# Hybrid encoder trunk on one core: the gated convolution inside the attention stage, its sums on GpSimd, its column tiles in another order

## The chip, the cores and the metric

The kernel runs on one core of one Trainium2 chip. Its engines are TensorE (PE; PEld is its weight load), VectorE (DVE), ScalarE (ACT), GpSimd (POOL) and SyncE (SP, which issues the DMAs here). The metric is the device time of one execution in microseconds (us), as the median of several runs.

## The reference

Two layers over 1024 positions of 1024 channels, float32. Each mixes three head groups side by side, then runs a convolutional gated MLP:

```python
h = rmsnorm(x, norm1_g); p = h @ w_in
q, k, v, su, sv, cb, cc, cx = split(p, (512, 128, 128, 256, 256, 256, 256, 256))
a_out = softmax_attention(rope(rmsnorm(q)), rope(rmsnorm(k)), v)      # 8 heads, 2 KV heads
g_out = su * (sg_w @ rmsnorm(sv) + sg_b)                              # chunks of 128 positions
c_out = cb * dwconv3(cc * cx, conv_w)                                 # 256 channels
x = x + concat(a_out, g_out, c_out) @ w_out
x = x + (silu(g) * u) @ ffn_w_down,   [g, u] = dwconv3(rmsnorm(x) @ ffn_w_up)
# dwconv3(x, w)[t] = x[t-1] * w[0] + x[t] * w[1] + x[t+1] * w[2]
```

The change concerns `c_out` alone: three projections (C = `cc`, X = `cx`, gate = `cb`) and a three-tap convolution along the positions.

## The kernel before

Every float32 product is made from high and low parts: an operand is split into `h` (a rounded copy) and `l` (the rest), and three matmuls hh, hl, lh add up in PSUM. `split` does this: the copy (L106 on ACT, L110 on POOL), then the subtraction (L117 on DVE or POOL).

**The attention stage.** Per layer there are 16 units `u` (128 queries by one of the two KV groups, four heads `r` each). `attention` (L654) writes TensorE's order out by hand, under a manual schedule for TensorE alone; a scheduler orders the other engines. In each of eight positions `kc` of a unit it issues: the transposes of the previous unit's probabilities (`att_T`, L622, four of 128x128 into a bank of the PSUM pair `pa`, split from there by ACT L626 and DVE L627); in positions 0, 1, 3 and 4 one head's scores (`att_scores`: matmuls L605 and L606, maximum on DVE L608, exponential on ACT L611, reciprocal on DVE L613, and the scaling of the probabilities by it on POOL, L614); some filler matmuls; and the product with V (L634, L635) of the hl pair made two positions earlier. The first transposes of a unit read all four heads of the unit before, so they need its fourth L614. DVE L649 and L650 end a unit's output.

**The filler** is the generator `conv_steps` (L454): the gated convolution's 288 matmuls of a layer (L301), one for each step. It goes over six column tiles of 128 channels, `order`, each as two halves of 512 positions, 24 matmuls a half, all into the one PSUM bank `pf`. For the channels j = 0, 1 the tiles come in turn as C, X, gate. A C half is copied out by ACT (L473) into `cc` (buffer G1); an X half is multiplied into it by DVE (L475), and after the second half `conv3` makes the three-tap sum: ACT L438 writes t = w1 * u, then DVE L439 and L443 add the two shifted products, each over 1023 positions in one instruction. A gate half is multiplied into t by DVE (L480). Steps are drawn at FILL: 16 ahead of unit 0, 32 in it, 12 in each unit 1 to 15, 24 in the unit 16 (which only transposes and multiplies with V), and the remaining 36 after it. So the second tile, X of channels 0, ends with unit 4; the fourth ends with unit 12; the fifth ends half-way through unit 16.

**Weights.** `cw_load` brings the next tile's 512 KB by DMA into buffer E5 (the first tile's into E8) and POOL splits them into G6/W0 or G7/W3 in turn. E5 is handed from one tile to the next, and after the last to a slice of the output projection's weights (`load_wo0`), whose second slice goes to G1, where `cc` has been. ACT and DVE or POOL split these slices into H0 and H1, the buffers of the probabilities, when attention has read them for the last time. SP issues DMAs in one queue, in the scheduler's order.

Of the kernel before, what the change touches and what calls it, by code (L numbers as in the profile page):

```python
# [10 lines left out]
AF = mybir.ActivationFunctionType  # L11
ALU = mybir.AluOpType
# [4 lines left out]
NT = 1024  # L17
# [5 lines left out]
C_K, C_SU, C_CB, C_CC, C_CX = 512, 768, 1280, 1536, 1792  # L23
# [33 lines left out]
class Trunk:  # L57
# [351 lines left out]
    def sg_half(self, half):  # L409
# [22 lines left out]
            nc.scalar.activation(B[:, kc, :], acc, AF.Copy)  # L432
        self.mB[half] = B

    def conv3(self, t, u, w):

        nc = self.nc
        nc.scalar.activation(t, u, AF.Copy, scale=w[1])  # L438
        nc.vector.scalar_tensor_tensor(  # L439
            out=t[:, 1:NT], in0=u[:, 0 : NT - 1], scalar=w[0], in1=t[:, 1:NT],  # L440
            op0=ALU.mult, op1=ALU.add,
        )
        nc.vector.scalar_tensor_tensor(  # L443
            out=t[:, 0 : NT - 1], in0=u[:, 1:NT], scalar=w[2], in1=t[:, 0 : NT - 1],
            op0=ALU.mult, op1=ALU.add,
        )
# [7 lines left out]
    def conv_steps(self, L, hT):  # L454

        nc = self.nc
        order = [(j, c) for j in range(2) for c in (C_CC, C_CX, C_CB)]
        self.mC = [None, None]
        W = {0: self.cw_load(L, order[0][1], 0)}
        for n, (j, c) in enumerate(order):  # L460
            if n + 1 < len(order):
                j2, c2 = order[n + 1]
                W[n + 1] = self.cw_load(L, c2 + j2 * P, n + 1)
            if c == C_CC:
                cc = self.S("G1")
            elif c == C_CX:
                t = self.mC[j] = self.S(("Z0", "Z1")[j])
            for half in range(2):
                s = slice(half * 512, half * 512 + 512)
                pm = self.acc("pf")  # L470
                yield from self.chan_mm_steps(pm, hT, half, W[n])
                if c == C_CC:
                    nc.scalar.activation(cc[:, s], pm, AF.Copy)  # L473
                elif c == C_CX:
                    nc.vector.tensor_tensor(out=cc[:, s], in0=pm, in1=cc[:, s], op=ALU.mult)  # L475
                    if half == 1:
                        w = [self.cst[:, 88 + 2 * k + j : 89 + 2 * k + j] for k in range(3)]
                        self.conv3(t, cc, w)
                else:
                    nc.vector.tensor_tensor(out=t[:, s], in0=pm, in1=t[:, s], op=ALU.mult)  # L480
                yield
# [800 lines left out]
```

## Time and profile before

| | |
|---|---|
| median of 3 runs | 2242.65 us (2241.32 to 2243.2) |
| profiled execution, its own time | 2240.78 us |
| its span (first to last instruction) | 2239.0 us |
| granted TensorE clock, mean | 0.998 |
| busy: PE / DVE / ACT / POOL | 99% / 68% / 49% / 51% of the span |
| attention stages | about 142 to 395 us and 1251 to 1506 us |

The busy shares are of the whole span; a stage can have another limit. The lists of waits say what ended the idle time of an engine; "A <- B: 6.6, 4, 2.0" is 6.6 us in all, four times, the longest 2.0 us.

### The profile page before, as it was taken

How to read it: one execution, taken by the hardware profiler on the slowest of the kernel's cores; microseconds unless marked ns; L12 is line 12 of the kernel's file. 1: busy time of each engine (PE TensorE's matmuls, PEld its weight loads, DVE VectorE, ACT ScalarE, POOL GpSimd, SP SyncE). 2: the span in 40 equal slices, each digit the busy share in tenths (PEclk: the TensorE clock that was granted, in tenths of full speed). 3: DMA queues.
4: the chain of work that ended last, by engine and by line, in shares of the span. 5: the costliest groups of instructions: out<-in, count | busy, mean ns of one | idle time of the engine just before them, and what ended most of it. 6: DMA issues, size and time to landing. Idle time of an engine off the chain costs nothing.

```text
span 2239.0 us, 29385 instructions
## 1 busy us (share of the span) xinstructions
PE 2206.4 (99%) x10590; PEld 1830.0 (82%) x10590; DVE 1530.1 (68%) x1953; ACT 1107.5 (49%) x1879; POOL 1130.9 (51%) x1028
## 2 busy tenths in 40 slices
PE   9999999999999999999999999999999999999999
PEld 7887887877888888888888878878788888888887
DVE  6568887278687777754735688872777777778554
ACT  4247776265454444433422467763555454444332
POOL 5463335587777777020443633356777777751100
PEclk9999999999999999999999999999999999999999
DMA  4110002223555453886520000032235554548754
GB/s 160 42 29 10 11 10 85 104 76 101 163 161 169 151 168 121 296 314 215 198 90 10 29 10 11 10 106 92 77 112 160 168 157 160 165 141 316 282 192 163
DMA packets 202019, 281.90 MB, mean 126 GB/s; under 512 B 15598, under 2 KB 121618, under 8 KB 201874
## 3 DMA queue, kind: packets, MB, share of 16 engines
q1 hardware_dynamic: 201874, 280.03, 37.2%
q8 instruction: 83, 1.36, 0.2%
q14 instruction: 62, 0.51, 0.1%
HBM read 199.77 MB, written 80.22 MB: 125 GB/s over the span
## 4 chain that ended last, share of the span: by engine, by line
PE 87%; DVE 5%; POOL 2%; DMA 2%; issue 2%; ACT 2%; SPq 0%; POOLq 0%; DVEq 0%; ACTq 0%
PE pa L860 18%; PE pf L860 9%; PE big L1059 8%; PE pa L1059 5%; PE pf L301 5%; PE pa L622 5%; PE po L860 4%; PE po L1059 3%; PE pf L1059 3%; PE big L606 3%; PE big L605 3%; PE po L634 2%; PE po L635 2%; PE pa L132 2%; PE pa L131 2%; PE pa L130 2%
## 5 line engine op out<-in xcount | busy, mean ns | idle before, releaser
L614 POOL TENSOR_SCALAR H<-H,rv 128x1024 f32<-128x1024 f32 x128 | 144.8, 1131 | 269.6 <-DVE rv L613 269.6
L860 PE MATMUL pa<-H,E 128*128 128x512 f32 x864 | 212.8, 390 | 1.4 <-DVE H L893 1.4
L106 ACT ACTIVATE E<-E 128x512 fp32r<-128x512 f32 (+1 forms) x207 | 128.5, 628 | 159.2 <-POOL E L848 69.8
L627 DVE TENSOR_TENSOR E<-pa,E 128x512 fp32r<-128x512 f32 x256 | 173.3, 688 | 48.1 <-ACT E L626 46.6
L117 POOL TENSOR_TENSOR E<-E,E 128x512 fp32r<-128x512 f32 (+1 forms) x120 | 176.0, 1471 | 51.0 <-ACT E L106 50.6
L626 ACT ACTIVATE E<-pa 128x512 fp32r<-128x512 f32 x256 | 152.9, 597 | 87.9 <-PE pa L622 86.6
L860 PEld LDWEIGHTS pa<-H,E 128*128 128x128 f32 x864 | 161.6, 188 | 35.7 <-DVE H L893 2.3
L106 ACT ACTIVATE G<-H 128x1024 fp32r<-128x1024 f32 (+1 forms) x116 | 114.1, 1008 | 143.3 <-PE big L1059 71.9
L117 DVE TENSOR_TENSOR G<-H,G 128x1024 fp32r<-128x1024 f32 (+1 forms) x86 | 104.6, 1220 | 109.4 <-ACT G L106 109.1
L622 PEld LDWEIGHTS pa<-ident,H 128*128 128x128 f32 x1024 | 127.4, 141 | 42.7 <-issue 4.7
L622 PE MATMUL pa<-ident,H 128*128 128x128 f32 x1024 | 154.3, 273 | 6.7 <-DVE E L627 6.6
L608 DVE TENSOR_REDUCE nm<-big 128x1 f32<-128x1024 f32 x128 | 155.6, 1216 | 6.3 <-PE big L606 6.2
L894 ACT ACTIVATE H<-pa 128x512 f32<-128x512 f32 x128 | 75.8, 593 | 166.4 <-PE pa L860 121.3
L611 ACT ACTIVATE H<-big,nm 128x1024 f32<-128x1024 f32 x128 | 142.4, 1113 | 18.0 <-DVE nm L608 17.9
L301 PE MATMUL pf<-H,G 128*128 128x512 f32 x320 | 130.4, 428 | 1.6 <-DVE Z L480 1.6
L439 DVE SCALAR_TENSOR_TENSOR big<-H,cst,big 128x1023 f32<-128x1023 f32 x44 | 56.6, 1287 | 102.2 <-ACT big L438 102.2
L117 DVE TENSOR_TENSOR E<-E,E 128x512 fp32r<-128x512 f32 (+1 forms) x92 | 97.3, 1066 | 39.3 <-ACT E L106 38.8
L860 PE MATMUL pa<-W,E 128*128 128x512 f32 x336 | 116.0, 394 | 0.8 <-ACT H L894 0.5
L106 ACT ACTIVATE G<-E 128x512 fp32r<-128x512 f32 (+2 forms) x110 | 58.5, 547 | 99.1 <-POOL E L848 29.8
L978 POOL TENSOR_TENSOR E<-E 128x512 f32<-128x512 f32 x26 | 35.3, 1360 | 140.0 <-DMA E<-in_ffn_w_down_dram 139.7
L860 PE MATMUL po<-H,E 128*128 128x512 f32 x408 | 104.4, 390 | 0.4 <-ACT E L106 0.4
L634 PE MATMUL po<-E,E 128*128 128x512 f32 x256 | 101.0, 394 | 2.2 <-DVE E L650 2.2
(400 smaller groups left out, 6353.5 us busy)
## 6 DMA issues: line engine op xcount, KB each, us to landing
H<-gdram SPq DMA_DIRECT2D x70, 512.0 KB, 5.6
gdram<-H SPq DMA_DIRECT2D x134, 256.0 KB, 2.4
E<-in_ffn_w_up_dram SPq DMA_DIRECT2D x66, 512.0 KB, 4.4
H<-tdram SPq DMA_DIRECT2D x40, 512.0 KB, 5.7
E<-in_w_in_dram SPq DMA_DIRECT2D x30, 512.0 KB, 3.9
H<-in_ffn_w_down_dram SPq DMA_DIRECT2D x30, 512.0 KB, 4.7
out_dram<-H SPq DMA_DIRECT2D x28, 512.0 KB, 2.9
E<-in_ffn_w_down_dram SPq DMA_DIRECT2D x26, 512.0 KB, 6.6
```

Source lines behind the costliest of these rows:

```text
L106: nc.scalar.activation(out, in_, AF.Copy)
L117: e.tensor_tensor(out=l, in0=src, in1=h.bitcast(F32), op=ALU.subtract)
L301: mm(acc, a[:, k, :], b, start=k + j == 0, stop=k == KC - 1 and j == 2)
L608: nc.vector.tensor_reduce(out=nm, in_=S, op=ALU.max, axis=AX.X, negate=True)
L611: nc.scalar.activation(p, S, AF.Exp, bias=nm, accum_out=sm)
L614: nc.gpsimd.tensor_scalar(out=p, in0=p, scalar1=rv, scalar2=1.0, op0=ALU.mult, op1=ALU.mult)
L622: nc.tensor.transpose(pt[:, r * P : (r + 1) * P], pu[:, r, kc * P : (kc + 1) * P], self.ident)
L626: nc.scalar.activation(hl[:, 0, :], pt, AF.Copy)
L627: nc.vector.tensor_tensor(out=hl[:, 1, :], in0=pt, in1=hl[:, 0, :].bitcast(F32), op=ALU.subtract)
L634: self.nc.tensor.matmul(O, v, hl[:, 0, :], start=kc == 0, stop=False)
L860: mm(out, w, x, start=first and k + j == 0, stop=k == 3 and j == 2, skip_group_check=True,)
L1059: nc.tensor.matmul(banks[j], p[:, n, s], r[:, n, :], start=first and n + q == 0 and m < 3, stop=last and n == w - 1 and q == 2, skip_group ...
```

## The change

A new function `conv3_pool` stands in for `conv3` in the attention stage: ACT still writes t = w1 * u, and GpSimd makes, for each half of the positions and each of the two outer taps, a scaled shifted copy in a temporary (buffer E5) and adds it to t, eight instructions instead of DVE's two. The tiles come as C, X, C, X, gate, gate. The second half of the first tile and of the last goes to a `pa` bank.

```diff
+    def conv3_pool(self, t, u, w):
+        self.nc.scalar.activation(t, u, AF.Copy, scale=w[1])
+        tmp = self.S("E5")
+        for a, b in ((0, 512), (512, NT)):
+            for o, k in ((-1, 0), (1, 2)):
+                lo, hi = max(a, -o), min(b, NT - o)
+                src, dst = tmp[:, lo:hi], t[:, lo:hi]
+                self.nc.gpsimd.tensor_scalar(
+                    out=src, in0=u[:, lo + o : hi + o], scalar1=w[k], scalar2=1.0,
+                    op0=ALU.mult, op1=ALU.mult,
+                )
+                self.nc.gpsimd.tensor_tensor(out=dst, in0=src, in1=dst, op=ALU.add)
...
-        order = [(j, c) for j in range(2) for c in (C_CC, C_CX, C_CB)]
+        order = [(j, c) for j in range(2) for c in (C_CC, C_CX)] + [(0, C_CB), (1, C_CB)]
...
-                t = self.mC[j] = self.S(("Z0", "Z1")[j])
+                self.mC[j] = self.S(("Z0", "Z1")[j])
+            t = self.mC[j]
...
-                pm = self.acc("pf")
+                pm = self.acc("pa" if half and n in (0, 5) else "pf")
...
-                        self.conv3(t, cc, w)
+                        self.conv3_pool(t, cc, w)
```

Lines behind the new function stand 16 later in the changed kernel (L614 is L630, L627 is L643). The order of three engines moves where the prediction speaks of it. On GpSimd, at the end of unit 4 of the first layer, before (H0 and H1 are the probabilities of even and odd units, E5 the raw weights):

```order
L614 TENSOR_SCALAR H0_404_2106<-H0_404_2106,rv_432_2210 128x1024
L110 TENSOR_SCALAR G7_447_2280<-E5_446_2278 128x1024
L117 TENSOR_TENSOR W3_448_2281<-E5_446_2278,G7_447_2280 128x1024
L614 TENSOR_SCALAR H1_439_2257<-H1_439_2257,rv_445_2275 128x1024
L614 TENSOR_SCALAR H1_439_2257<-H1_439_2257,rv_456_2310 128x1024
L614 TENSOR_SCALAR H1_439_2257<-H1_439_2257,rv_465_2344 128x1024
L614 TENSOR_SCALAR H1_439_2257<-H1_439_2257,rv_471_2368 128x1024
```

and now (Z0 is t, G1 is u, cst holds the taps):

```order
L443 TENSOR_SCALAR E5_439_2251<-G1_269_1539,cst_125_645 128x512
L447 TENSOR_TENSOR Z0_298_1667<-E5_439_2251,Z0_298_1667 128x511
L447 TENSOR_TENSOR Z0_298_1667<-E5_439_2251,Z0_298_1667 128x512
L443 TENSOR_SCALAR E5_439_2251<-G1_269_1539,cst_125_645 128x512
L443 TENSOR_SCALAR E5_439_2251<-G1_269_1539,cst_125_645 128x511
L447 TENSOR_TENSOR Z0_298_1667<-E5_439_2251,Z0_298_1667 128x512
L447 TENSOR_TENSOR Z0_298_1667<-E5_439_2251,Z0_298_1667 128x511
L630 TENSOR_SCALAR H1_440_2264<-H1_440_2264,rv_446_2282 128x1024
L630 TENSOR_SCALAR H1_440_2264<-H1_440_2264,rv_458_2318 128x1024
L630 TENSOR_SCALAR H1_440_2264<-H1_440_2264,rv_467_2352 128x1024
L110 TENSOR_SCALAR G7_448_2287<-E5_447_2285 128x1024
L630 TENSOR_SCALAR H1_440_2264<-H1_440_2264,rv_473_2376 128x1024
```

Seven of the convolution's eight instructions stand in one block between units 4 and 5 (the first stands two units earlier), and the split of the next weights has moved from ahead of unit 5's scalings to either side of the fourth of them. The same rows come at unit 12, and both again in layer 1.

On VectorE, at the same place before:

```order
L475 TENSOR_TENSOR G1_269_1539<-pf_372_1968,G1_269_1539 128x512
L627 TENSOR_TENSOR E8_438_2244<-pa_437_2239,E8_438_2244 128x512
L439 SCALAR_TENSOR_TENSOR Z0_298_1667<-G1_269_1539,cst_125_645,Z0_298_1667 128x1023
L608 TENSOR_REDUCE nm_443_2271<-big_442_2266 128x1
L627 TENSOR_TENSOR E6_441_2263<-pa_440_2258,E6_441_2263 128x512
L443 SCALAR_TENSOR_TENSOR Z0_298_1667<-G1_269_1539,cst_125_645,Z0_298_1667 128x1023
L649 TENSOR_TENSOR E1_373_1972<-po_420_2166,ot_450_2288 64x2x128
L650 TENSOR_TENSOR E1_373_1972<-po_420_2166,ot_450_2288 64x2x128
```

and now:

```order
L491 TENSOR_TENSOR G1_269_1539<-pf_372_1968,G1_269_1539 128x512
L643 TENSOR_TENSOR E8_438_2244<-pa_437_2239,E8_438_2244 128x512
L624 TENSOR_REDUCE nm_444_2278<-big_443_2273 128x1
L643 TENSOR_TENSOR E6_442_2270<-pa_441_2265,E6_442_2270 128x512
L665 TENSOR_TENSOR E1_373_1972<-po_420_2166,ot_452_2296 64x2x128
L666 TENSOR_TENSOR E1_373_1972<-po_420_2166,ot_452_2296 64x2x128
```

The two sums are gone between the product (L475, now L491) and the unit's maxima and subtractions; nothing else changes place.

On ScalarE, at the end of unit 15, before (H0 is free once unit 15 has transposed it):

```order
L626 ACTIVATE E6_852_3948<-pa_851_3943 128x512
L106 ACTIVATE H0_874_4119<-E5_876_4121 128x1024
L626 ACTIVATE E7_854_3962<-pa_853_3957 128x512
L647 ACTIVATE ot_855_3970<-po_834_3870 64x256
L648 ACTIVATE ot_855_3970<-po_834_3870 64x256
L626 ACTIVATE E8_857_3980<-pa_856_3975 128x512
```

and now:

```order
L106 ACTIVATE H0_876_4133<-E5_878_4135 128x1024
L106 ACTIVATE H0_876_4133<-G1_879_4137 128x1024
L642 ACTIVATE E7_856_3979<-pa_855_3974 128x512
L663 ACTIVATE ot_857_3987<-po_836_3887 64x256
L664 ACTIVATE ot_857_3987<-po_836_3887 64x256
L642 ACTIVATE E8_859_3997<-pa_858_3992 128x512
```

The second weight slice's copy (from G1) has come forward, ahead of unit 16's first copy out of `pa`; before, it waited for `conv3` of the channels 1 to release G1.

## Rows read from the trace of the kernel before

**Rows 1.** The page: busy time of each engine, and the chain's shares by engine.
```profile
PE 2206.4 (99%) x10590; PEld 1830.0 (82%) x10590; DVE 1530.1 (68%) x1953; ACT 1107.5 (49%) x1879; POOL 1130.9 (51%) x1028
...
PE 87%; DVE 5%; POOL 2%; DMA 2%; issue 2%; ACT 2%; SPq 0%; POOLq 0%; DVEq 0%; ACTq 0%
```
**Rows 2.** Waits of TensorE, whole span: us in all, times, longest.
```profile
PE pa L622 <- DVE E L627: 6.6, 4, 2.0
PE po L634 <- DVE E L650: 2.2, 2, 1.1
PE pf L301 <- DVE Z L480: 1.6, 2, 0.8
PE pf L301 <- ACT G L473: 1.4, 2, 0.7
```
**Rows 3.** Timeline of DVE around unit 4's end: start, us, line, tiles, idle before.
```profile
212.21 0.69 DVE L475 TENSOR_TENSOR G<-pf,G 128x512 f32<-128x512 f32 x1
214.12 2.95 DVE L439 SCALAR_TENSOR_TENSOR Z<-G,cst,Z 128x1023 f32<-128x1023 f32 x1 [0.62 <-ACT Z L438]
216.99 1.21 DVE L608 TENSOR_REDUCE nm<-big 128x1 f32<-128x1024 f32 x1
218.13 0.68 DVE L627 TENSOR_TENSOR E<-pa,E 128x512 fp32r<-128x512 f32 x1
218.72 1.27 DVE L443 SCALAR_TENSOR_TENSOR Z<-G,cst,Z 128x1023 f32<-128x1023 f32 x1
```
**Rows 4.** Timeline of PE, first transposes of unit 5 and those of position 2.
```profile
212.94 0.60 PE L622 MATMUL pa<-ident,H 128*128 128x128 f32 x4
218.95 0.63 PE L622 MATMUL pa<-ident,H 128*128 128x128 f32 x4 [1.96 <-DVE E L627]
```
**Rows 5.** Stretch after the same place in layer 1: length, busy times, clock, DMA, GB/s.
```profile
1331.00:1335.00 4.00, 3.85 (x12) 3.10 (x13) 3.38 (x7) 1.69 (x3) 1.13 (x1) 0.57 0.01 4
```
**Rows 6.** Timeline of GpSimd: fourth scaling of unit 12, four of unit 13.
```profile
326.11 1.12 POOL L614 TENSOR_SCALAR H<-H,rv 128x1024 f32<-128x1024 f32 x1 [0.34 <-DVE rv L613]
333.62 1.14 POOL L614 TENSOR_SCALAR H<-H,rv 128x1024 f32<-128x1024 f32 x1 [2.88 <-DVE rv L613]
336.01 1.13 POOL L614 TENSOR_SCALAR H<-H,rv 128x1024 f32<-128x1024 f32 x1 [1.25 <-DVE rv L613]
338.29 1.13 POOL L614 TENSOR_SCALAR H<-H,rv 128x1024 f32<-128x1024 f32 x1 [1.15 <-DVE rv L613]
340.24 1.13 POOL L614 TENSOR_SCALAR H<-H,rv 128x1024 f32<-128x1024 f32 x1 [0.82 <-DVE rv L613]
```
**Rows 7.** Timeline of PE: first transposes of units 13 and 14.
```profile
327.68 0.60 PE L622 MATMUL pa<-ident,H 128*128 128x128 f32 x4
341.77 0.60 PE L622 MATMUL pa<-ident,H 128*128 128x128 f32 x4
```
**Rows 8.** Durations by line: ns min/median/max, first and last start.
```profile
L627 DVE TENSOR_TENSOR E<-pa,E x256: 669/692/694, 159.2 to 1494.5; 128x512 fp32r<-128x512 f32 x128
L439 DVE SCALAR_TENSOR_TENSOR Z<-G,cst,Z x4: 2367/2674/2958, 214.1 to 1488.5; 128x1023 f32<-128x1023 f32 x4
```
**Rows 9.** Groups of GpSimd instructions, shapes apart: busy us, mean ns, idle before.
```profile
L614 POOL TENSOR_SCALAR H<-H,rv 128x1024 f32<-128x1024 f32 x128 | 144.8, 1131 | 269.6 <-DVE rv L613 269.6
L117 POOL TENSOR_TENSOR W<-E,G 128x1024 fp32r<-128x1024 f32 x10 | 24.0, 2404 | 0.5
L978 POOL TENSOR_TENSOR E<-E,E 128x512 f32<-128x512 f32 x8 | 15.7, 1962 | 0.6
```
**Rows 10.** Timeline of ACT around unit 4's end.
```profile
212.94 1.15 ACT L438 ACTIVATE Z<-G,cst 128x1024 f32<-128x1024 f32 x1 [0.53 <-DVE G L475]
```
**Rows 11.** Timeline of ACT at the end of unit 15.
```profile
368.48 1.05 ACT L106 ACTIVATE H<-E 128x1024 fp32r<-128x1024 f32 x1
```
**Rows 12.** The page: DMA issues, KB each, median us to landing.
```profile
E<-in_w_in_dram SPq DMA_DIRECT2D x30, 512.0 KB, 3.9
E<-in_ffn_w_down_dram SPq DMA_DIRECT2D x26, 512.0 KB, 6.6
```

## The prediction

> **What bounds the kernel now.** First the page's busy times and chain: TensorE is busy 2206.4 of 2239.0 us and holds 87% of the chain [rows 1]. It is the bound, and a change is worth only the idle time (some 33 us in all) that it gives back or adds. So the next view is TensorE's own list of waits, from which I take the four lines that belong to the filler or to the attention around it [rows 2]: 6.6 us in four waits of the transposes for DVE's subtraction L627, 2.2 us in two of the product with V for DVE's L650, 1.6 us in two of the filler for DVE's gate product, 1.4 us in two for ACT's copy of a C half. Both bank waits come from `pf` being a single bank. The sum is 11.8 us, half in each layer.
>
> DVE's timeline names the cause of the first two lines [rows 3]: after unit 4 the first sum L439 takes 2.95 us and the second, L443, 1.27 us, and the maximum and the subtraction that unit 5 needs stand in the queue between and behind them. TensorE, which began unit 5 at 212.94, waits 1.96 us for the bank of position 2 [rows 4]. The other pair of such waits lies in unit 16, where the sums of the channels 1 come. In layer 1 the same stall is followed by 4 us at a mean granted clock of 0.57, that is, mostly at 1.2 instead of 2.4 GHz, with TensorE nearly always busy [rows 5]: 4.00 x (1 - 0.57) = 1.7 us more. In layer 0 the clock stays at full speed after it. So 11.8 + 1.7 = 13.5 us can be had in the profiled execution.
>
> **The change part by part.**
> *DVE loses the four pairs of sums.* Nothing on DVE takes their place, and the product ahead of them stays. The 8.8 us of the first two lines go, if nothing else makes L627 late. What is left ahead of it is ACT's scaling of 1.15 us, which stays where it was [rows 10]: it holds unit 5's first copy by some 0.4 us, and the bank concerned is asked for again only two positions later. I take no stall from it; at worst its whole length in each of four places, 4.6 us.
>
> *GpSimd gains eight instructions for each of the four sums.* No row of before shows them, so they are bounded. A scaling of 128x512: half of the 1.13 us of L614 with 1024 elements, 0.57; at most 1.13. An add of 128x512: half of the 2.40 us of the weights' subtraction of 1024 elements, 1.20; at most the 1.96 us of the slowest group of this shape [rows 9]. I take the lower ones, since the weights' subtraction runs in this very stage. The whole is 4 x (0.57 + 1.20) = 7.1 us; one scaling stands two units earlier, where GpSimd is idle for several us between units. The block of seven starts when the second half's product is done, which is when the next unit starts (product at 212.21 for 0.69 us, unit at 212.94 [rows 3, 4]). Call that T. The adds need ACT's scaling, done at T + 1.2. So the block ends at T + 1.2 + 4 x 1.20 + 2 x 0.57 = T + 7.1.
>
> What stands behind it are the next unit's four scalings L614, and TensorE needs the fourth for the first transposes of the unit after. Unit 13 of before shows when they come without disturbance [rows 6, 7]: with T = 327.68, at T + 5.9, 8.3, 10.6 and 12.6; the fourth ends at T + 13.7 and unit 14 starts at T + 14.1. Behind the block the first runs from 7.1 to 8.3, 1.2 us late; the second starts at 8.3, on time. The delay is caught up before it reaches TensorE.
>
> *The weights' split moves.* Its copy L110 now stands between the third and the fourth scaling, and its raw data cannot be loaded before the block has left E5. SP issues that DMA at T + 7.1 and it lands 3.9 us later [rows 12], at T + 11.0; the third scaling ends at 11.7, so the copy (1.1 us) runs 11.7 to 12.8 and the fourth scaling 12.8 to 13.9, 0.2 us before unit 14 needs it. So this just fits: the cover is the third scaling, and it holds as long as an add stays under some 1.35 us. At 1.42 us an add the stall would be about 0.2 us in each of four places. I take 0.1 us each, 0.4 in all. The other weights are split as before, up to four units ahead of use. In layer 0 and 1 alike SP now also loads the slice for G1 ahead of the last tile's weights; G1 comes free with the block's last scaling, 2.4 us earlier, so that DMA is half through when the second starts.
>
> *The tiles' order.* C of channels 1 writes `cc` half a tile after the first sum has read it for the last time; the gates come tens of us after their sums. No wait comes of it, and the matmuls are the same in number. G1 is released at unit 12 rather than in unit 16, so the output projection's second slice is there early. Its copy of 1.05 us now stands ahead of unit 16's first copy on ACT [rows 11], which comes 0.8 us late; the bank is asked for again at position 2, where L627 ends just in time. I take 0.3 us in each layer, 0.6 in all; at worst 1.05 each.
>
> *Two halves in `pa`.* The first tile's second half runs in unit 0, when no transposes use `pa`; the last half runs after the attention, when their last bank has long been read. Both bank waits go, 1.6 + 1.4 = 3.0 us. Before, six matmuls of the output projection stood ahead of the last product with V; now they stand behind the filler, and that product comes right when its L627 ends. I take 0.1 us a layer, 0.2 in all.
>
> *Sum:* 13.5 - 0.4 - 0.6 - 0.2 = 12.3 us. From the profiled execution's own 2240.78 us this makes 2228.5. The median of the runs is 1.87 us above that execution, so the forecast is 2230.4, said as 2230.5.
>
> A rule of the Trainium skill speaks against the change. "GPSIMD Engine Reference", section "Engine selection", gives elementwise work on a tile to VectorE, since GpSimd is about twice as slow for operations with two inputs. No run here shows the ratio for this operation; the rows agree in direction, as the subtraction L627 of 512 elements takes 0.69 us on DVE [rows 8] and half of the weights' 2.40 us is 1.20 [rows 9]. By that rule the change loses wherever the sums are waited for; by the rows GpSimd has the time and DVE has not. The last rival is what it would look like.
>
> **The rivals.**
> *Half of it stays.* DVE is still the engine that TensorE nearly waits for, and ACT's scaling and the product come at the same moment as before; a stall of about 1 us could be left at each of the four places, and 0.5 us at each of two bank waits. For it: L439 itself ran at 2.37 to 2.96 us [rows 8] where the second sum took 1.27 [rows 3], so two engines working at once can cost each other time, and GpSimd now works exactly there. Against it: L627 took between 0.669 and 0.694 us in all 256 cases [rows 8], beside GpSimd's splits too. Time: 2230.5 + 5 = 2235.5.
>
> *The stall is not the sums'.* If the DVE queue was late for another reason (the product or ACT's scaling), only the bank waits go: 2242.65 - 3.0 = 2239.6, within 0.2% of before, about what a measurement of this kernel can tell from no change. Against it: rows 3 show the queue filled by the two sums, 4.2 of 7 us.
>
> *GpSimd becomes the bound, and the kernel slower.* The mechanism is the fourth scaling behind the copy that waits for its DMA. With adds at 1.96 us the block ends at T + 10.2; with a DMA of 6.6 us, as in the slower rows [rows 12], the data land at T + 16.8; copy and scaling at 1.13 each end at T + 19.1, 5.0 us after unit 14 (or 6) should start. Four places make 20.0 us: 2240.78 - 13.5 + 20.0 + 1.87 = 2249. It decides from 3.4 us a place (13.5 / 4). Against it: both must be at their far ends at once, and the queues are empty of other DMAs there.
>
> **How the numbers follow.** The forecast has a chance of 0.72, with a range of its own from 2227 (nothing new added and one more half-speed stretch of 1.7 us gone) to 2233; half of it 0.14; the same 0.08; slower 0.06. Clock stretches can come or go with any small shift, 1.7 us each. The range of 8 in 10 is 2226.5 to 2237. Faster by over 0.2% (4.5 us): 0.72 + 0.14 = 0.86; within: 0.08; slower: 0.06.
>
> **What would show it.** In TensorE's waits the four lines are gone or under 1 us together; DVE's timeline has maximum and subtraction right behind the product; GpSimd's block of seven takes 6 us with adds of 1.2 us; the fourth scaling of units 5 and 13 ends before TensorE's first transposes of units 6 and 14; the clock after unit 4 of layer 1 is full. The prediction is wrong if transposes wait for L614 (now L630), if L627 still waits behind something after the product, or if the time stands above 2237.

## The result and the profile after

The changed kernel takes 2225.33 us (median of 6 runs, 2223.99 to 2226.26), the kernel before beside it 2243.19 us: a ratio of 0.992, 95% interval 0.9907 to 0.9933. The gain is 17.9 us where the prediction's sum was 12.3; the time lies 1.2 us below the predicted range. The direction and the mechanism held, the size did not.

The page of the changed kernel, busy times and then the chain by engine, answering to [rows 1]:

```profile
PE 2202.3 (99%) x10590; PEld 1829.1 (82%) x10590; DVE 1511.4 (68%) x1945; ACT 1106.9 (50%) x1879; POOL 1156.9 (52%) x1060
...
PE 85%; POOL 4%; DVE 3%; DMA 3%; issue 2%; ACT 1%; SPq 0%; POOLq 0%; DVEq 0%; ACTq 0%
```

GpSimd is 26 us busier and DVE 19 us less. TensorE's waits of the changed kernel (us in all, times, longest) begin with rows of other stages; the four lines of [rows 2] are gone:

```profile
PE pa L876 <- DVE Z L117: 3.7, 3, 1.7
PE big L280 <- DVE Z L262: 3.4, 5, 1.4
PE po L226 <- POOL ident masks.py:199: 1.7, 1, 1.7
```

DVE's timeline around unit 4's end (start, us, line, tiles; idle before in brackets), answering to [rows 3]. In the changed kernel L491 is the product, L624 the maximum, L643 the subtraction:

```profile
211.68 0.69 DVE L491 TENSOR_TENSOR G<-pf,G 128x512 f32<-128x512 f32 x1
212.28 0.68 DVE L643 TENSOR_TENSOR E<-pa,E 128x512 fp32r<-128x512 f32 x1
213.97 1.23 DVE L624 TENSOR_REDUCE nm<-big 128x1 f32<-128x1024 f32 x1 [1.00 <-PE big L622]
215.11 0.68 DVE L643 TENSOR_TENSOR E<-pa,E 128x512 fp32r<-128x512 f32 x1
```

DVE now idles for TensorE here, not the reverse: nothing stands between the product and what TensorE needs. The first transposes of units 5 and 6, answering to [rows 4]:

```profile
212.40 0.60 PE L638 MATMUL pa<-ident,H 128*128 128x128 f32 x4
...
226.53 0.60 PE L638 MATMUL pa<-ident,H 128*128 128x128 f32 x4
```

The unit takes 14.13 us. The stretch that answers to [rows 5] (length, TensorE's busy time, clock, DMA share, GB/s), and above it one in unit 5 of layer 0:

```profile
217.00:222.00 5.00, 5.00 (x29) 1.00 0.12 29
...
1331.00:1335.00 4.00, 4.00 (x26) 1.00 0.47 129
```

GpSimd's timeline from the block to the fourth scaling, answering to [rows 6]; L443 and L447 are the sums, L630 the scalings, L110 and L117 the weights' split:

```profile
212.46 0.70 POOL L443 TENSOR_SCALAR E<-G,cst 128x512 f32<-128x512 f32 x1 [0.50 <-DVE G L491]
213.70 2.54 POOL L447 TENSOR_TENSOR Z<-E,Z 128x511 f32<-128x511 f32 x2 [0.54 <-ACT Z L437]
216.22 1.38 POOL L443 TENSOR_SCALAR E<-G,cst 128x512 f32<-128x512 f32 x2
217.58 2.54 POOL L447 TENSOR_TENSOR Z<-E,Z 128x512 f32<-128x512 f32 x2
220.10 2.23 POOL L630 TENSOR_SCALAR H<-H,rv 128x1024 f32<-128x1024 f32 x2
223.02 1.12 POOL L630 TENSOR_SCALAR H<-H,rv 128x1024 f32<-128x1024 f32 x1 [0.70 <-DVE rv L629]
224.11 1.05 POOL L110 TENSOR_SCALAR G<-E 128x1024 fp32r<-128x1024 f32 x1
225.14 1.14 POOL L630 TENSOR_SCALAR H<-H,rv 128x1024 f32<-128x1024 f32 x1
226.25 2.40 POOL L117 TENSOR_TENSOR W<-E,G 128x1024 fp32r<-128x1024 f32 x1
```

The block ends 7.7 us after unit 5 began, and the fourth scaling at 226.28, 0.25 us before unit 6's first transposes, which read it, begin without a wait.

### The profile page after: what moved, and what is told of

It is laid out like the page before. It is cut to its first block, busy times and chain, and to the rows that moved or that the text cites. A ratio compares the mean times of both kernels' runs of the same rounds, so it can differ in the third digit from the quotient of the medians.

```text
span 2223.4 us, 29441 instructions
## 1 busy us (share of the span) xinstructions
PE 2202.3 (99%) x10590; PEld 1829.1 (82%) x10590; DVE 1511.4 (68%) x1945; ACT 1106.9 (50%) x1879; POOL 1156.9 (52%) x1060
## 4 chain that ended last, share of the span: by engine, by line
PE 85%; POOL 4%; DVE 3%; DMA 3%; issue 2%; ACT 1%; SPq 0%; POOLq 0%; DVEq 0%; ACTq 0%
PE pa L876 17%; PE pf L876 8%; PE big L1075 8%; PE pa L1075 5%; PE pa L638 5%; PE pf L301 5%; PE po L876 4%; PE big L622 3%; PE big L621 3%; PE po L650 3%; PE po L651 3%; PE po L1075 2%; PE pf L1075 2%; PE pa L132 2%; PE pa L130 2%; PE pa L131 2%
## 5 line engine op out<-in xcount | busy, mean ns | idle before, releaser
L630 POOL TENSOR_SCALAR H<-H,rv 128x1024 f32<-128x1024 f32 x128 | 144.6, 1130 | 221.8 <-DVE rv L629 221.8
L643 DVE TENSOR_TENSOR E<-pa,E 128x512 fp32r<-128x512 f32 x256 | 173.4, 688 | 52.2 <-ACT E L642 50.8
L117 POOL TENSOR_TENSOR E<-E,E 128x512 fp32r<-128x512 f32 (+1 forms) x120 | 176.5, 1475 | 53.0 <-ACT E L106 52.6
L117 DVE TENSOR_TENSOR G<-H,G 128x1024 fp32r<-128x1024 f32 (+1 forms) x86 | 105.0, 1224 | 110.3 <-ACT G L106 109.9
L624 DVE TENSOR_REDUCE nm<-big 128x1 f32<-128x1024 f32 x128 | 155.7, 1216 | 8.1 <-PE big L622 8.0
L627 ACT ACTIVATE H<-big,nm 128x1024 f32<-128x1024 f32 x128 | 142.4, 1112 | 12.3 <-DVE nm L624 12.2
L117 DVE TENSOR_TENSOR E<-E,E 128x512 fp32r<-128x512 f32 (+1 forms) x92 | 96.3, 1055 | 38.2 <-ACT E L106 38.2
L301 PE MATMUL pf<-H,G 128*128 128x512 f32 x288 | 120.1, 431 | 0.0
L994 POOL TENSOR_TENSOR E<-E 128x512 f32<-128x512 f32 x26 | 37.0, 1425 | 140.2 <-DMA E<-in_ffn_w_down_dram 139.9
L864 POOL TENSOR_TENSOR E<-E 128x512 f32<-128x512 f32 x66 | 100.5, 1524 | 3.1
```

Of the source, the lines that this page charges most:

```text
L117: e.tensor_tensor(out=l, in0=src, in1=h.bitcast(F32), op=ALU.subtract)
L301: mm(acc, a[:, k, :], b, start=k + j == 0, stop=k == KC - 1 and j == 2)
L624: nc.vector.tensor_reduce(out=nm, in_=S, op=ALU.max, axis=AX.X, negate=True)
L627: nc.scalar.activation(p, S, AF.Exp, bias=nm, accum_out=sm)
L630: nc.gpsimd.tensor_scalar(out=p, in0=p, scalar1=rv, scalar2=1.0, op0=ALU.mult, op1=ALU.mult)
L643: nc.vector.tensor_tensor(out=hl[:, 1, :], in0=pt, in1=hl[:, 0, :].bitcast(F32), op=ALU.subtract)
```

## The experiments

Each changes the kernel before or after in one thing, except that "old order, free buffers" and the whole-width kernels with added work change two. "Idle" is TensorE's waits within 140 to 460 and 1240 to 1575 us (the attention stages and the output projections behind them), summed over the rows of one profile of that kernel (three profiles of before give 11.7, 10.9 and 11.3, so differences under 1 us say nothing); the clock is the mean granted one over all its executions ("before": 90 of them beside these runs, whose medians lie between 2242.5 and 2243.8 us).

| kernel | median us (runs) | ratio to before, interval | idle us | clock |
|---|---|---|---|---|
| before | 2243.2 | 1 | 11.7 | 0.9974 |
| after | 2225.3 (6) | 0.992 [0.9907, 0.9933] | 0 | 0.9993 |
| after again | 2225.9 (4) | 0.9929 [0.9914, 0.9944] | 0 | 0.9990 |
| GpSimd only | 2244.6 (10) | 1.0004 [0.9994, 1.0013] | 12.5 | 0.9954 |
| order only | 2249.9 (7) | 1.003 [1.0019, 1.0041] | 14.8 | 0.9963 |
| bank only | 2238.7 (9) | 0.9975 [0.9966, 0.9985] | 9.1 | 0.9972 |
| after without GpSimd | 2246.0 (10) | 1.0011 [1.0001, 1.0021] | 11.7 | 0.9960 |
| after without order | 2244.2 (10) | 1.0012 [1.0002, 1.0021] | 12.6 | 0.9947 |
| after without bank | 2230.9 (4) | 0.9946 [0.9932, 0.9961] | 3.3 | 0.9988 |
| scalings twice | 2224.9 (4) | 0.9924 [0.9909, 0.9939] | 0 | 0.9995 |
| scalings four times | 2234.8 (6) | 0.9966 [0.9955, 0.9978] | 6.6 | 0.9988 |
| whole width | 2240.3 (10) | 0.9987 [0.9978, 0.9997] | 10.0 | 0.9970 |
| old order, free buffers | 2235.2 (6) | 0.9971 [0.9959, 0.9982] | 5.9 | 0.9978 |
| after, more work, first try | 2241.4 (10) | 0.999 [0.998, 0.9999] | 3.2 | 0.9990 |
| whole width, work, first try | 2241.6 (10) | 0.999 [0.998, 0.9999] | 3.2 | 0.9993 |
| after, 10 us more work | 2237.0 (7) | 0.9974 [0.9962, 0.9985] | 0 | 0.9991 |
| whole width, same work | 2237.7 (8) | 0.9976 [0.9966, 0.9986] | 0 | 0.9996 |

### The parts, alone and taken away

**GpSimd only** (edit to the kernel before): `- self.conv3(t, cc, w)` `+ self.conv3_pool(t, cc, w)`.

> Sums on GpSimd alone; tiles in the old order, all halves in the one bank. My theory (the three parts add up, the sums' stall is most of it): the waits of L622 for DVE L627 and of L634 for L650 after unit 4 go in both layers (6.1 us of idle time, some 1.1 us of slow restart, 1.7 us of clock), the bank waits of 3.0 us stay, and the sums of the channels 1 still come in unit 16, where GpSimd's block of 7.7 us now delays the output projection's splits: about 2236, 7 us under before. Rival (the new tile order gives nothing): 2228 to 2229, that is the full change plus the bank waits. Second rival (the gain is the order's): 2241 or more.

It gained nothing, and my theory fell. The second rival's time is met, but not its reason, since the order alone gains nothing either (next run). DVE's sums no longer stop the transposes, but a larger wait came up in the output projection, for a weight slice's low part (the last two rows are the bank waits):

```profile
PE pa L131 <- DVE H L117: 9.1, 2, 4.7
PE pf L301 <- DVE Z L496: 1.9, 2, 1.0
PE pf L301 <- ACT G L489: 1.4, 2, 0.7
```

**Order only**: `- order = [(j, c) ... for c in (C_CC, C_CX, C_CB)]` `+ order = [... (C_CC, C_CX)] + [(0, C_CB), (1, C_CB)]`.

> Tile order C, X, C, X, gate, gate alone; sums on DVE, one bank. My theory: the stall of unit 16 (1.3 us a layer) moves to unit 13 and grows to the 3.6 us that unit 5 pays, so 2 us a layer slower, perhaps another half-speed stretch of 1.7 us: 2245 to 2250, slower than before by 2 to 6 us. Rival (the order itself pays, by freeing G1 and DVE at the stage's end): 2238 to 2241.

As the theory said, with a loss of 6.6 us just above the 2 to 6 expected. The second pair of sums moves from unit 16 to unit 13 and stops the transposes there:

```profile
PE pa L638 <- DVE E L643: 7.9, 4, 2.0
PE po L650 <- DVE G L666: 2.1, 2, 1.1
PE po L650 <- DVE E L666: 1.7, 2, 1.1
```

**Bank only**: `- pm = self.acc("pf")` `+ pm = self.acc("pa" if half and n in (0, 5) else "pf")`.

> The second bank for two halves alone. My theory: the two kinds of bank waits go, 3.0 us of idle time in all and up to 1 us of restart: 2239 to 2240.5. Rival (the banks' waits are covered by the waits behind them, or the pair pa is short of a buffer): 2243, no change.

The two bank rows are gone, the sums' rows stay; the gain is 4.6 us for 3.0 us of rows, a little more than the theory's.

**After without GpSimd**: `- self.conv3_pool(t, cc, w)` `+ self.conv3(t, cc, w)`.

> The change without GpSimd: new order and second bank, sums on DVE. My theory: order's loss of 2 to 6 us less the bank's gain of 3 to 4: 2242 to 2247. Rival (order and bank are what pays): 2232 or less.

2246.0 us, as the theory said: without GpSimd's sums the order and the bank together lose 2.8 us.

**After without order** (the tiles in the old order, the rest as after):

> The change without the new tile order: sums on GpSimd, second bank. My theory: GpSimd's second block of 7.7 us falls into unit 16, in front of the low parts that the output projection's first block needs, and the last tile's gate product waits for it: 2230 to 2236, 5 to 10 us above the full change. Rival (the order is indifferent): 2225 to 2226, as the full change.

My theory fell here, as in the first experiment. The same wait dominates:

```profile
PE pa L131 <- DVE H L117: 10.1, 2, 5.2
PE pa L130 <- ACT H L106: 2.6, 2, 1.6
```

**After without bank**: `- pm = self.acc("pa" if half and n in (0, 5) else "pf")` `+ pm = self.acc("pf")`.

> The change without the second bank: new order, sums on GpSimd, all halves in the one bank. My theory: the two bank waits come back, 3 to 4 us: 2228 to 2229.5. Rival (with DVE relieved the gate product comes at once and only the wait at the start stays): 2226.5 to 2227.

The bank's two rows are back (1.6 and 1.4 us, and one of 0.3 us for GpSimd's L630) and cost 5.6 us, more than my theory's 3 to 4. So the parts don't add: GpSimd alone is worth nothing, the order alone is a loss, and together with the bank they bring 17.9. With the buffers as they are, the order is what makes GpSimd's sums usable: without it the changed kernel is 18.8 us slower.

**Old order, free buffers** asks why. In the old order the sums of channels 1 run in unit 16, and E5 (their temporary) and G1 are what the output projection's first weights are loaded to. Edit to "after without order": `WO_RAW = ("E5", "G4", "G0", "W1")` for `("E5", "G1", ...)`, and `tmp = ("E5", "G5")[j]`.

> The old order of tiles (C, X, gate, C, X, gate) with sums on GpSimd and the second bank, as in the run without the new order, but the second sum's temporary in another buffer (G5) and the output projection's second slice loaded raw to G4, so that neither of these two waits for the sums in unit 16. Theory (the old order loses because E5 and G1 are held until the sums end and the weights come late): most of that loss goes, 2228 to 2236 us, and the wait of TensorE for H's subtraction L617-like of 10 us shrinks under 4 us. Rival (the sums' place alone on GpSimd's queue, in front of the last units' scalings and the weights' splits, costs it, whatever the buffers): still 2240 to 2246 us with the same wait.

The wait for H's subtraction of 10.1 us is gone, and the kernel 9.0 us faster than "after without order". Shown: holding those buffers was about half of the loss (9.0 of 18.8 us), not most of it as the theory had it; the two were freed together, so their shares are not known. Of the rest, the profile shows two new rows in the output projection:

```profile
PE pf L130 <- DVE Z L496: 3.2, 1, 3.2
PE pa L130 <- ACT G L106: 2.7, 1, 2.7
```

The second is a weight slice again. The first names the last gate's product, which reads the sums: in this trace DVE idled 3.4 us, in four waits, ahead of these products (L496) until GpSimd's add L447 was done. That wait was not tried by itself.

### How much room GpSimd has

**Scalings twice** and **four times**: in `conv3_pool`, `+ for _ in range(2):` (or 4) ahead of `gpsimd.tensor_scalar(out=src, ...)`; the value is the same.

> Each GpSimd scaling of the sums is done twice (the same values again), which adds 4 x 0.69 = 2.8 us to each sum, three of the four in the block of seven. Theory (room between block and the transposes two units on just suffices, because the weights' copy is put behind the fourth scaling): no row of TensorE waiting for the hidden's scaling L631, or under 1 us in all; time 2225 to 2228 us. Rival (after stands at the very edge, 0.25 us before a stall): the 2.1 us that the block is longer arrive in full less 0.25 at each of four places, 4 x 1.8 = 7.4 us, time about 2232 us and a row of TensorE waiting for GpSimd in H.

> The full change with each of the eight scaled copies made four times over (the same values; only GpSimd's time grows, by 4 x 3 x 0.69 = 8.3 us a sum). My theory (GpSimd's room between the units is just used up): twelve copies, four adds, the weights' copy and its DMA, and four scalings end some 22 us after the unit's start instead of 13.9, so the transposes of the unit after wait some 8 us at each of four places, plus half-speed stretches: 2255 to 2265. Rival (GpSimd has ample room): under 2228.

Twice is free, though it adds 2.8 us to a sum and after had 0.25 us left: in this run the scheduler put one scaling L631 between the sums and the weights' copy L110 behind the fourth. So it does not show what a longer block costs in after's own order. Four times costs 9.4 us, in a row that the prediction's last rival speaks of, at a fraction of its price (my 2255 us assumed that the order stays; in this trace scalings L631 stand between the parts of the sums):

```profile
PE pa L639 <- POOL H L631: 6.6, 7, 1.2
```

**Whole width**: `- for a, b in ((0, 512), (512, NT)):` `+ for a, b in ((0, NT),):`.

> The sums on GpSimd in one piece of 1023 columns each: four instructions a sum in place of eight. Theory (what counts is that the sums are off DVE; the halves are no part of the gain): 2224.5 to 2227 us, no waits of TensorE in the attention. Rival (halves matter, since with the first scaling of a whole width waiting for the second half of the product the block grows by one scaling of about 1.3 us and by the overhead of nothing, and after had 0.25 us left): four stalls of about 0.5 to 1 us, 2227 to 2229 us, and TensorE waits for L630 (the hidden's scaling).

Neither: 2240.3 us. GpSimd's timeline of this kernel, and then TensorE's:

```profile
217.02 2.40 POOL L447 TENSOR_TENSOR Z<-E,Z 128x1023 f32<-128x1023 f32 x1
219.41 2.27 POOL L630 TENSOR_SCALAR H<-H,rv 128x1024 f32<-128x1024 f32 x2
223.45 1.06 POOL L110 TENSOR_SCALAR G<-E 128x1024 fp32r<-128x1024 f32 x1 [1.77 <-DMA E<-in_w_in_dram]
224.47 1.13 POOL L630 TENSOR_SCALAR H<-H,rv 128x1024 f32<-128x1024 f32 x1
225.57 2.37 POOL L117 TENSOR_TENSOR W<-E,G 128x1024 fp32r<-128x1024 f32 x1
227.91 1.12 POOL L630 TENSOR_SCALAR H<-H,rv 128x1024 f32<-128x1024 f32 x1
```

```profile
226.13 0.49 PE L638 MATMUL pa<-ident,H 128*128 128x128 f32 x3
229.09 0.33 PE L638 MATMUL pa<-ident,H 128*128 128x128 f32 x1 [2.47 <-POOL H L630]
```

The sums end 7.4 us after unit 5 began (at 212.00), 0.3 us sooner than in halves. But now the copy, which waits 1.77 us for its DMA, stands ahead of the third scaling and the subtraction of 2.37 us ahead of the fourth; TensorE waits 2.47 us for it, four times. This is the prediction's third rival, brought about by the order and not by slow adds. In halves the split stands one place further back in the scheduler's order, and by the two timelines that is what they are worth here. A whole-width kernel with after's order on GpSimd was not run; that the wait is what costs is shown below, where work that covers it takes the loss away.

### What a stall costs

Over the kernels with idle in these stages the time above after is 1.4 to 1.8 times the idle (9.4/6.6 at the least, 20.7/11.7 at the most; before 17.9/11.7). The prediction had 13.5 for 11.8, 1.14 times.

**After, more work** puts TensorE to work for as long as "whole width" lets it wait. The first try, edit to after in `att_T`, position 6 of units 5 and 13:

```
+        for _ in range(busy):      # 11 in these four places
+            nc.tensor.matmul(pt, self.qT[:, 0, :], self.kT[0][0][:, 0, :], start=True, stop=True)
```

> The changed kernel with 11 extra 128x512 matmuls, all to a PSUM bank that is overwritten right behind them, ahead of the transposes of position 6 in units 5 and 13 (four places in two layers). Matmuls of this shape follow each other every 0.233 us in the trace of after, so TensorE gets 2.56 us more work at each place, 10.25 us in all, about as long as the waits of the whole-width run (10.0 us), but with TensorE busy. Theory (a stall costs about half as much again as its row says because TensorE stands still: restart and half-speed stretches): added work costs its own length and no more, 2225.3 + 10.25 = 2235.6 us (2234.5 to 2236.5), with a spread of the runs as small as after's. Rival (anything that lengthens this stage by 10 us costs 15): 2240 us.

> The whole-width version of the sums with the same 11 extra matmuls in units 5 and 13, that is, ahead of the places where TensorE waited 2.5 us for GpSimd; GpSimd's order is the same. Theory: the waits are covered by work (a row of TensorE waiting for H under 1.5 us in all), the time is that of the changed kernel plus the extra work, 2235.6 us (2234.5 to 2237.5): less than the whole-width version without the work (2240.3), though TensorE has 10.25 us more to do. Rival (the whole width loses by something else than TensorE standing still): 2240.3 to 2250 us.

2241.4 us (10 runs) and 2241.6 (10): both above the expectation, and inconclusive, since the extra matmuls wait for the next unit's queries, a stall of its own:

```profile
224.15 2.80 PE L638 MATMUL pa<-E,G 128*128 128x512 f32 x11 [0.83 <-DVE G L604]
```

So again, with operands that have long been there (`self.kT[0][0][:, 0, 0:P]` for `self.qT[:, 0, :]`):

> The changed kernel with the 11 extra matmuls at the same four places (11 x 0.233 = 2.56 us each, 10.25 us in all), but of operands that have long been there (parts of the keys), so that no wait of 0.8 us for the queries comes with them, as it did in the first try. Theory (a stall costs half as much again as its row because TensorE stands still): work costs its own length: 2225.3 + 10.25 = 2235.6 us; with the slightly slower first matmul and the spread, 2234.5 to 2237. Rival (10 us more in this stage, busy or not, cost 15): 2240 us or more.

> The whole-width version with the same extra matmuls of operands that have long been there, just ahead of the places where it waited 2.5 us. Theory: no waits of TensorE for H are left (under 1.5 us in all), and the time is that of the run with the changed kernel and the same work, 2234.5 to 2237.5 us: 10.25 us more work, yet 3 to 6 us less than the whole-width version without it (2240.3). Rival: the waits stay or the time is 2240 us or more.

TensorE's timeline of the first of them, then its two attention stages:

```profile
222.69 2.68 PE L638 MATMUL pa<-E 128*128 128x512 f32 x11
225.21 0.60 PE L640 MATMUL pa<-ident,H 128*128 128x128 f32 x4
```

```profile
140.00:460.00 320.00, 319.99 (x1689) 266.29 (x1688) 215.72 (x341) 204.38 (x404) 169.23 (x175) 1.00 0.14 47
1240.00:1575.00 335.00, 334.98 (x1759) 278.65 (x1759) 224.67 (x362) 208.84 (x417) 181.54 (x190) 1.00 0.14 46
```

The columns are the length, the busy time of PE, PEld, DVE, ACT and POOL, the clock, DMA share and GB/s. No idle, full clock, and 11.7 us more than after for 10.1 us of work (4 x 2.52, from 222.69 to the transposes at 225.21): 1.2 times, where 10.0 us of waiting cost 15.0. Even the 1.2 holds other things: the profiled execution is 11.0 us longer than after's, and besides the work it has 2.6 us more of waits outside these stages (19.2 against 16.6 us) and one stretch at 1.2 GHz less. The whole-width version with the work added is 2.7 us faster than without it (the intervals 0.9966 to 0.9986 and 0.9978 to 0.9997 overlap a little), 0.2 us above what I had set as the upper end. The rival falls: it is standing still that costs more than its row. The whole width with its wait covered is within 0.7 us of after with the same work, so its loss was that wait and little else.

**What fills the difference: the clock.** A second and third profile of before, a second of whole width and of after:

> The kernel before, unchanged, for a second profile. My theory of the 2.4 us by which the median of before lies above its profiled execution: other executions have one or two half-speed stretches more (1.7 us each) behind the stalls of the attention stage, so this profile shows three or more, or else as many at other places; the waits of TensorE are the same to 0.3 us. Rival (the difference lies outside the span or in the waits): the same two stretches, and a span and waits that differ.

> The kernel before, a third profile. Theory: same waits of 11 to 12 us in the attention stage; two to four stretches of 3.4 us at 1.2 GHz, each behind a wait of over 1 us in the attention or the output projection, and a time of 2240.8 plus 1.7 us for each stretch beyond two.

> The whole-width version again, for a second profile: its first was the fastest of ten executions (2235.6 us against a median of 2240.3) and showed little time at 1.2 GHz. Theory: same waits of 10.0 us; an execution near the median has three or more stretches of 3.4 us at 1.2 GHz behind the waits (mean granted clock 0.996 to 0.998). Rival: the clock is 0.999 again at 2240 us, and the rest is something else.

> The changed kernel again, unchanged. Theory: 2225.3 us (2224 to 2226.5); its profile shows none or one stretch of 3.4 us at 1.2 GHz (mean granted clock 0.998 to 1.0), where the two profiles of the kernel before show two and three; a rival by which such stretches come anywhere at random: two or three of them here too, and a time 2 to 4 us longer in that execution.

Before took 2242.56 and 2242.89 us, whole width 2241.93 against 2235.63 in its first profile, after 2228.1 in the profiled one of its four. Apart from the last microseconds of the span, the second and third profile of before each have three stretches at 1.2 GHz (one behind unit 5's stall in layer 0, two in a row behind that of layer 1), where the first had one behind the stall of layer 1 and one at 502 us. So the number came as expected; the idle of 10.9 us in the second is not the same to 0.3. After's 2228.1 has one stretch, so it is not the clock that makes it 2.9 us longer than its first profile: its waits outside these stages sum to 19.5 us against 16.6. Stretches of the third profile of before, ahead of the stall in unit 5, over it, and behind it:

```profile
212.00:217.00 5.00, 5.00 (x29) 1.00 0.00 0
217.00:222.00 5.00, 1.92 (x10) 1.00 0.36 105
222.00:226.00 4.00, 4.00 (x14) 0.57 0.00 0
226.00:230.00 4.00, 4.00 (x25) 1.00 0.00 0
```

TensorE is busy 1.92 of 5 us, and then for 4 us at a granted clock of 0.57, mostly 1.2 GHz: 14 matmul records where 25 fit in the next 4 us. The first profile of before had none of this here, only in layer 1 [rows 5]. Whole width, second profile and then the first, at the same wait of unit 6:

```profile
226.00:230.00 4.00, 2.67 (x16) 1.00 0.00 0
230.00:234.00 4.00, 2.89 (x8) 0.61 0.48 135
```

```profile
226.00:229.00 3.00, 0.62 (x5) 1.00 0.00 0
229.00:233.00 4.00, 3.91 (x21) 1.00 0.46 131
```

The same wait (2.45 and 2.47 us) is followed by the lower clock in one execution and not in the other. The second profile has three such places (behind the waits of units 6 and 14 in layer 0 and of one in layer 1) and one more at about 21 us, where after's second profile has its only one; the first has one, in layer 1. Three more at 4 x (1 - 0.57) = 1.7 us make 5.1 of the 6.3 us between the two executions.

## Why the prediction was wrong

By its own steps:

- *What bounds the kernel; which lines go.* Right for the change as a whole. All four lines are gone, DVE's maximum and subtraction stand behind the product, the clock after unit 4 of layer 1 is full. But the prediction gave the order no worth and took 0.6 us off for it, and the first experiments show that, with the buffers as they are, the 8.8 us it booked for the sums are not had without it.
- *What filled DVE's queue.* The prediction took the first sum's 2.95 us as the sum's own, and named the gap to the second sum's 1.27 [rows 3] only as a risk to the change. In all four places of the kernel before, GpSimd's subtraction of a weights' split runs beside the first sum, which ends 1.08 us after it; the second sum of unit 5 ran while GpSimd was idle. GpSimd's timeline there:

```profile
213.59 2.40 POOL L117 TENSOR_TENSOR W<-E,G 128x1024 fp32r<-128x1024 f32 x1
222.79 1.14 POOL L614 TENSOR_SCALAR H<-H,rv 128x1024 f32<-128x1024 f32 x1 [6.79 <-DVE rv L613]
```

  So some 1.7 us of the first sum (2.95 - 1.27, an estimate) may be its neighbour's, against a wait of 1.96 us in that unit. A kernel that leaves the sums on DVE and moves the split aside was not run; how much of the gain it would have had stays open.
- *GpSimd's cost.* An add took 1.29 us (forecast 1.20), a scaling 0.69 to 0.72 (0.57), the block ended at T + 7.7 (T + 7.1). Each was sized a little low, and it still fitted, with 0.25 us left. The third scaling ended at T + 11.7 and the fourth at T + 13.9, both as forecast. Whether 0.25 us is an edge in this order was not tested, since the scalings done twice came in another; "after without bank" waited 0.3 us for L630 at one place, so it may be.
- *Deductions of 0.4, 0.6 and 0.2 us.* None came: no row of TensorE for L630, for the first copy of unit 16, or for the last product with V. That is 1.2 us. The 0.4 does not follow from the prediction's own times either: with adds of 1.42 us the block ends at T + 8.0, the data land at 11.9 and the fourth scaling ends at 14.1, just when unit 14 starts.
- *The stall's price.* This is the step that failed: the sum took idle rows at their length plus one half-speed stretch of 1.7 us, those of one profile, and carried "the median is 1.87 us above the execution" over as a constant. The clock's mean over 90 executions of before is 0.9974, over after's ten 0.9992, so a typical execution loses 5.8 us (2243 x 0.0026) before and 1.8 after: 4.0 us, not 1.7, go with the stalls. The profiled execution of before had two such stretches; the two profiled later had three each, 1.7 us more, which is most of the 1.87 us. The same account holds for whole width: 2240 x 0.0030 = 6.7 us, 4.9 more than after, are all of the 5.0 us by which its price (15.0) exceeds its idle (10.0). It does not close for every kernel: idle and clock together are some 4 us too much for "after without order" and 3 too little for "order only".
- *What no row holds.* At full clock the difference is then 17.9 - 4.0 = 13.9 us for 11.8 us of rows. Unit 5 took 17.77 us before, from 212.94 [rows 4] to the row below, and 14.13 after, 3.64 us less, where its two idle rows hold 1.96 and 1.1; 0.58 us are in no row. The two profiled executions alone say much the same: of the 15.6 us between their spans, 11.7 are idle here and 1.7 one more stretch at 1.2 GHz, waits elsewhere take off 0.7, and some 3 are in no row. This may be a restart behind the wait, but whole width shows nothing of the kind, as just said; so what the 2.1 us are stays open.

TensorE's timeline of the kernel before, first transposes of unit 6:

```profile
230.71 0.60 PE L622 MATMUL pa<-ident,H 128*128 128x128 f32 x4
```

Together: 1.2 + (4.0 - 1.7) + 2.1 = 5.6 us, and 12.3 + 5.6 = 17.9.

Of the rivals, "half of it stays" fell with the rows, and "not the sums'" with "GpSimd only", where DVE's rows go with the sums alone. The third is real, as whole width shows, but wasn't met: the copy stood behind the third scaling.

The rule weighed in the prediction (the Trainium skill, "GPSIMD Engine Reference", section "Engine selection") says that GpSimd is about twice as slow as VectorE for elementwise work with two inputs. The trace agrees on the price: an add of 128x512 took 1.29 us on GpSimd, a subtraction of that shape 0.69 us on DVE [rows 8]. It does not agree on the choice: GpSimd took 8.0 us a sum where DVE took 4.2 [rows 3], and the kernel became faster, since TensorE waited for DVE's queue and not for GpSimd's.

## What to carry to other kernels

Price a stall of the bounding engine above its idle row: here 1.4 to 1.8 times, and count lower-clock stretches over many executions, not from one profile. When work is moved to an idler engine, look at which buffers it holds until it ends and at the order the scheduler then gives to that engine's queue; here both decided more than the durations. When one instruction takes twice its usual time, look at what ran beside it before moving it. A part that loses alone can be what makes another part pay.

## What the hardware showed

Waits of some 2 to 3 us of TensorE were followed by 1.2 GHz in one execution and by full speed in another of the same kernel, at the same place. So the times of one kernel differ: whole width 2235.6 to 2243.2 us over ten runs, the changed kernel 2223.9 to 2228.1 over ten. Idle is not all of that spread, since the whole width with its wait covered still took 2235.7 to 2240.6 over eight.

GpSimd beside DVE did not slow what reads PSUM: L643 took 0.671 to 0.694 us in all 256 cases after, as L627 before [rows 8]. DVE's first sum, which reads u and t from SBUF, took 2.37 to 2.96 us in four places where GpSimd's subtraction of two such operands had begun before it, and the second 1.27 where GpSimd was idle [rows 3, 8].
